# Second context pair's projections split around the first pair's masked products, and products ahead of transposes

## Chip, cores and metric

The kernel runs on one core of a Trainium2 chip. The metric is device time of one execution in microseconds (us), median of the runs shown. Engines are called PE (TensorE, matrix products), DVE (VectorE), ACT (ScalarE), POOL (GpSimd) and SP (SyncE, which issues loads).

## What is computed

A backbone of two layers over 512 latent tokens of width 1024 with a prefix of 256 context tokens. Layer 0 mixes with a bidirectional RWKV-7 recurrence over 16 heads of width 64, next to a gated short convolution; layer 1 is a convolution module. The change touches the recurrence over the context tokens, whose state at the end starts the recurrence over the latents:

```python
def wkv_scan(S0, r, decay, k, v, kk, a, reverse):
    def step(S, inp):
        r_t, w_t, k_t, v_t, kk_t, a_t = inp
        sa = jnp.einsum("bhvk,bhk->bhv", S, -kk_t)
        S = (S * w_t[:, :, None, :]
             + sa[..., None] * (kk_t * a_t)[:, :, None, :]
             + v_t[..., None] * k_t[:, :, None, :])
        return S, jnp.einsum("bhvk,bhk->bhv", S, r_t)
    ...
# k, v are projections of the normed tokens (h @ w_in), mixed with both neighbours:
    k = k + (centred_shift(k) - k) * mu_rkv[1]
    v = v + (centred_shift(v) - v) * mu_rkv[2]
```

Each scan runs forward and backward. Outside the recurrence, the conditioning needs `s @ mod_w[i] + mod_b[i]`.

## The kernel before

The scan is worked in chunks of 64 tokens. Two heads of 64 fill the 128 partitions, so 16 heads make 8 head pairs `p`. For the context (4 chunks), two head pairs are taken together: four states `sts[0]` to `sts[3]`, called context pairs here; context pair `b` holds head pairs `2b` and `2b+1`. The latents follow as eight more states. In names `c0` is context pair 0, `l0` latent pair 0, `z` (0, 1) the direction.

Steps of a context pair, by function:

- `prep_ctx`: key and value projections of both head pairs. `project` does the context tokens (PSUM tile `pc…`, 24 products of 256 columns) and then the latents with the same weights (`pl…`, 24 products of 512 columns; the result is stored in DRAM by POOL for later). Weights arrive as float32 and are split into a high and a low part (ACT cast `wh…`, DVE subtraction `wl…`), hence three products for each. `shifted` clears the PSUM tile: ACT L405, DVE L406 and L408. The tags `mm0` and `mm1` take turns, one bank each, so `pck3` takes the bank of `pck2`.
- `light`: decay, key normalisation and the operands `AR` and `BK` of both directions, on ACT and DVE.
- `heavy`: by letters. A, the masked products `pac…` of AR and BK (PE), cleared through the mask into E by DVE (L646); B, transposes `pbc…` of BK (PE), copied to BKt by ACT (L659); N, copies of parts of E to Nt (ACT, L665). A string in `HEAVY` gives their order: first entry for context pairs, second for latent pairs. `pv` turns the values (`pvc…`). A and B use the tag `at`, two banks in all.
- `solve`: an inverse by 31 rank-one steps on DVE (L697, L703, L705), then `merge`: DVE transposes `kdmc` and `amc`, and small products `uh<-amc` and `uh<-kdmc` on PE that complete E.
- `chain_ctx`: the recurrence over chunks (`zoc…`, `uh…`).

`rest()` is a side job in 17 steps, called between other steps: it loads pieces of `mod_w` (POOL) and multiplies them (`mpb…`, `uh<-mwr`); after the eighth and the last product `rested` copies, transposes (`mr…`, L948) and adds. `fills` writes projections that no pair needs yet (`plr…`, `pza…`); they stand between the pairs' steps.

The order on each engine is not the order of the code: a scheduler at build time takes instructions by priority, which follows the code, and by when it expects operands to be ready. Each engine then runs its list strictly in that order and waits where an operand or a buffer is missing. Buffers come from pools by tag; a tile waits for the last reader of the one whose place it takes.

In the code, the second context pair was prepared after the first one's merge:

## Time and profile before

| | |
|---|---|
| median of 3 runs | 1410.81 us (1405.18 to 1412.49) |
| profiled execution | 1408.22 us |
| its span | 1406.5 us |
| PE busy | 1344.4 us, 96% |
| DVE, ACT busy | 979.9 us (70%), 746.7 us (53%) |
| granted PE clock, mean | 0.986 of full |

The span is what the hardware profiler saw from the first to the last instruction; the time also holds start and end around it. The four context pairs fill the time from about 110 to 440 us, latent pairs follow to 940 us, then layer 1. A row of the timeline gives the start, the duration, engine, line, operation, output<-inputs, and in brackets the idle time before it and what ended that. PE rows overlap since products are pipelined: what a block takes is read from start to start.

### The profile page before, as it was taken

Reading aid. Unit: us, or ns where it says so; the run is one execution under the profiler, and the core shown is the slowest. Engines: PE = TensorE matmul, PEld = TensorE weight load, DVE = VectorE, ACT = ScalarE, POOL = GpSimd, SP = SyncE. Lnnn points to the kernel's source line nnn. Section 1 sums busy time; section 2 is a strip of 40 time slices with the busy share of each in tenths; the row PEclk is TensorE's granted clock in tenths of the full one; section 3 lists DMA queues with packets and bytes.
Section 4 is the critical chain, followed back from the end, with each engine's and each line's share of the span. In section 5 each row is a group of like instructions: output and inputs, shape, how many; then the busy total and the mean of one; then the engine's idle time right before and its main releaser. Section 6 shows DMA issues by size and latency. Waiting matters only on the chain. (4 is left out here: it accounts for less than half of the span.)

```text
span 1406.5 us, 29747 instructions
## 1 busy us (share of the span) xinstructions
PE 1344.4 (96%) x11921; PEld 1001.9 (71%) x11921; DVE 979.9 (70%) x2290; ACT 746.7 (53%) x1516; POOL 127.5 (9%) x263
## 2 busy tenths in 40 slices
PE   5898999999999998999999999999999999999998
PEld 1665767777767766666666666678777787788886
DVE  2775687877899789999999988556754644534333
ACT  4746355645757464665757656446752432453322
POOL 4022210001011001101011000010000000000000
PEclk9998899999999999999999999999999999999999
DMA  9864441223233222222222222459712312133222
GB/s 335 233 201 150 149 129 58 68 91 89 76 110 97 83 62 84 78 71 84 63 87 75 64 59 86 160 184 326 253 32 89 120 45 75 61 105 101 94 93 88
DMA packets 137707, 158.55 MB, mean 113 GB/s; under 512 B 15503, under 2 KB 104223, under 8 KB 137449
## 3 DMA queue, kind: packets, MB, share of 16 engines
q1 hardware_dynamic: 121104, 106.47, 24.2%
q0 software_dynamic: 15856, 49.12, 10.8%
q8 instruction: 94, 1.54, 0.4%
q10 hardware_dynamic: 608, 1.06, 0.2%
q14 instruction: 45, 0.37, 0.1%
HBM read 138.33 MB, written 18.28 MB: 111 GB/s over the span
## 5 line engine op out<-in xcount | busy, mean ns | idle before, releaser
L57 PE MATMUL o<-wh,y 128*128 128x512 f32 x248 | 79.6, 397 | 0.0
L703 DVE TENSOR_TENSOR xtmpl<-Xl,Yl 128x126 f32<-128x126 f32 (+22 forms) x248 | 62.1, 250 | 3.0
L705 DVE TENSOR_TENSOR Yl<-Yl,xtmpl 128x126 f32<-128x126 f32 (+22 forms) x248 | 62.0, 250 | 2.9
L1212 ACT CAST ah<-a 64x512 fp32r<-64x512 f32 x32 | 19.8, 618 | 74.1 <-DVE a L1207 73.8
L57 PE MATMUL zol<-UV,E 64*64 64x64 f32 (+1 forms) x1024 | 54.0, 221 | 0.0
L57 PE MATMUL pal<-ARl,BKl 64*128 64x128 f32 x512 | 46.7, 304 | 7.3 <-DVE E L646 6.1
L57 PEld LDWEIGHTS o<-wh,y 128*128 128x128 f32 x248 | 45.9, 188 | 9.5
L57 PE MATMUL zol<-Hl,ARl 64*64 64x64 f32 x896 | 50.2, 230 | 1.2 <-DVE Hl L818 0.9
L811 ACT COPY UV<-uh 64x128 f32<-64x128 f32 x128 | 33.2, 260 | 33.0 <-PE uh L57 26.7
L57 PEld LDWEIGHTS zol<-Hl,ARl 64*64 64x64 f32 x896 | 35.0, 133 | 21.4 <-issue 17.4
L57 PE MATMUL o<-wl,y 128*128 128x512 f32 x124 | 49.3, 397 | 1.0 <-DVE wl L130 1.0
L57 PEld LDWEIGHTS pal<-ARl,BKl 64*128 64x128 f32 x512 | 36.8, 197 | 18.0 <-issue 6.6
L130 DVE TENSOR_TENSOR wl<-wr,wh 128x1024 fp32r<-128x1024 f32 x28 | 34.2, 1222 | 20.8 <-ACT wh L129 20.7
L57 PEld LDWEIGHTS uh<-UV,BKt 128*64 128x64 f32 x704 | 26.3, 137 | 30.8 <-ACT UV L811 24.9
L1207 DVE TENSOR_TENSOR a<-pu,a 128x512 f32<-128x512 f32 x16 | 11.0, 690 | 49.2 <-PE pu L57 46.9
L646 DVE TENSOR_TENSOR E<-pal,maskE 128x512 f32<-128x512 f32 x64 | 43.1, 684 | 2.3 <-PE pal L57 2.0
L57 PEld LDWEIGHTS zol<-UV,E 64*64 64x64 f32 (+1 forms) x1024 | 42.4, 136 | 2.5 <-ACT UV L811 2.0
L1164 DVE SCALAR_TENSOR_TENSOR pr<-px,dbe,What 119x512 f32<-119x512 f32 x32 | 22.6, 746 | 26.6 <-PE px L57 26.6
L129 ACT CAST wh<-wr 128x1024 fp32r<-128x1024 f32 x28 | 29.6, 1057 | 19.4 <-DMA wr<-in_ev_w_out_dram 10.1
L57 PE MATMUL uh<-UV,BKt 128*64 128x64 f32 x704 | 36.3, 232 | 3.6 <-ACT UV L811 2.4
L818 DVE SCALAR_TENSOR_TENSOR Hl<-uh,PCl,HPl 128x64 f32<-128x64 f32 x112 | 26.4, 276 | 17.1 <-PE uh L57 7.2
L57 PEld LDWEIGHTS uh<-Ol,E 64*64 64x64 f32 x512 | 19.9, 133 | 25.3 <-ACT Ol L805 18.9
(980 smaller groups left out, 4206.2 us busy)
## 6 DMA issues: line engine op xcount, KB each, us to landing
wr<-in_ev_w_out_dram SPq DMA_DIRECT2D x28, 512.0 KB, 5.2
mwr<-in_mod_w_dram POOLq DMA_DIRECT2D x28, 256.0 KB, 4.0
ectx<-in_mod_w_dram SPq DMA_DIRECT2D x12, 512.0 KB, 7.2
wrv<-in_ev_w_in_dram SPq DMA_DIRECT2D x16, 256.0 KB, 3.0
ectx<-in_mod_w_dram POOLq DMA_DIRECT2D x16, 256.0 KB, 4.2
wrr<-in_ev_w_in_dram SPq DMA_DIRECT2D x16, 256.0 KB, 2.9
wrza<-in_ev_w_in_dram SPq DMA_DIRECT2D x16, 256.0 KB, 2.9
wrcg<-in_ev_w_in_dram SPq DMA_DIRECT2D x16, 256.0 KB, 2.8
```

The lines of the kernel that those rows point to most:

```text
L57: env["pe"] = T.matmul(o, lhsT, rhs, start=start, stop=stop)
L129: S.copy(hi, raw)
L130: env["lo"].tensor_tensor(out=lo, in0=raw, in1=hi, op=ALU.subtract)
L646: st["ev"].append(V.tensor_tensor(out=E[:, h, z * NLAT + c0 : z * NLAT + c0 + m, :], in0=pas[h], in1=maskE[:, z * (1 + h) : z * (1 + h) + ...
L703: V.tensor_tensor(out=tv, in0=X[:, :i, i : i + 1].to_broadcast([P, i, m]), in1=Y[:, i : i + 1, c0:].to_broadcast([P, i, m]), op=ALU.mult)
L705: V.tensor_tensor(out=Y[:, :i, c0:], in0=Y[:, :i, c0:], in1=tv, op=ALU.add)
L811: u_ = S.copy(UV[ZR[1 - h], i : 2 * nch - i : 2 * nch - 1 - 2 * i, ZR[h]], uh[ZR[1 - h], 0:2, :])
L818: h_ = V.scalar_tensor_tensor(out=Hn[:, z, :], in0=uh[:, 2 + z, :], scalar=PC[z][:, i : i + 1], in1=HP[:, z, :], op0=ALU.mult, op1=ALU.add)
L1164: V.scalar_tensor_tensor(out=pr[s][:NPROD], in0=px[s][:NPROD], scalar=dbe[:, 0:1], in1=What[:, n * 512 : n * 512 + 512], op0=ALU.add, op1= ...
L1207: V.tensor_tensor(out=a, in0=pp[1], in1=a, op=ALU.mult)
L1212: S.copy(ahl[s][hr], a[hr])
```

## The change

The call that prepares the second context pair is split in two: the keys (`kinds=(1,)`) are written ahead of the first pair's `heavy`, the values (`kinds=(2,)`) behind its `solve`. For every context pair, `heavy` writes A and N ahead of B.

```diff
-HEAVY = ("BAN", "ANBV")
+HEAVY = ("ANB", "ANBV")
...
     light(sts[0])
+    sts.append(prep_ctx(1, rest, kinds=(1,), inner=rest))
     heavy(sts[0])
     sts[0]["pv"]()
     solve(sts[0])
+    prep_ctx(1, rest, st=sts[1], kinds=(2,), inner=rest)
     merge(sts[0])
-    sts.append(prep_ctx(1, rest, inner=rest))
     rest()
```

What this makes of the engines' lists is shown at three places. Rows that repeat are left out.

First, PE where the first pair's `heavy` stands; `plk2` is the last key projection of head pair 2 over the latents, `pck3` that of head pair 3 over the context, `pbc00…` and `pbc01…` the transposes of directions 0 and 1, `pac00…` and `pac01…` the products. Before:

```order
L57 MATMUL plk2_1335<-hlh_117,wlk21_1284 128x512
L57 MATMUL mpb_1365<-ectx_121,s2_71 2x512 x4
L621 MATMUL pbc001_1027<-ident_60,BKc00_988 128x64
...
L621 MATMUL pbc011_1047<-ident_60,BKc01_1018 128x64
...
L57 MATMUL pck3_1387<-hctx_120,whk30_1376 128x256 x2
L57 MATMUL pck3_1387<-hctx_120,wlk30_1377 128x256
L57 MATMUL pac0001_1067<-ARc00_987,BKc00_988 128x64
...
L57 MATMUL pac0101_1087<-ARc01_1017,BKc01_1018 128x64
...
L57 MATMUL pvc0_1110<-ctr_106,vc0_635 64x64 x16
L948 MATMUL mr0_1321<-ident_60,mrow0_1320 128x128 x2
```

And now:

```order
L948 MATMUL mr0_1069<-ident_60,mrow0_1068 128x128 x2
L57 MATMUL plk2_1083<-hlh_117,whk21_1031 128x512
...
L57 MATMUL mpb_1113<-ectx_121,s2_71 2x512 x4
L57 MATMUL pac0001_1213<-ARc00_987,BKc00_988 128x64
...
L57 MATMUL pck3_1135<-hctx_120,whk30_1124 128x256 x2
...
L57 MATMUL plk3_1171<-hlh_117,whk30_1124 128x512
...
L57 MATMUL pac0101_1233<-ARc01_1017,BKc01_1018 128x64
...
L57 MATMUL pcv2_1397<-hctx_120,whv20_1386 128x256 x2
...
L621 MATMUL pbc001_1257<-ident_60,BKc00_988 128x64
...
L621 MATMUL pbc011_1277<-ident_60,BKc01_1018 128x64
...
L57 MATMUL pvc0_1296<-ctr_106,vc0_635 64x64 x16
```

The products of direction 0 now come first, the whole of `pck3` and `plk3` stands between them and those of direction 1, and the transposes stand within the value projection `pcv2`; the `mr` transposes stand within `plk2`.

The same place on DVE, from the first direction's BK on. Before:

```order
L596 TENSOR_TENSOR BKc_988<-kdc_982,iPc_977 128x8x64
L561 SCALAR_TENSOR_TENSOR Pc_1005<-scm,sg 128x528
L130 TENSOR_TENSOR wlv_1464<-wrv_1462,whv_1463 128x512
L588 SCALAR_TENSOR_TENSOR ARc_1017<-kkc_960,Pc_1005 128x8x64
...
L595 SCALAR_TENSOR_TENSOR BKc_1018<-ac_1002,iPc_1007 128x8x64
L406 SCALAR_TENSOR_TENSOR kc_1275<-pck_1288,hmu,kc_1275 128x255
...
L408 SCALAR_TENSOR_TENSOR kc_1275<-pck_1288,hmu,kc_1275 128x255
L408 SCALAR_TENSOR_TENSOR lk_1360<-plk_1335,hmu,lk_1360 128x511
L646 TENSOR_TENSOR ectx<-pac_1067,maskE 128x512
...
L646 TENSOR_TENSOR ectx<-pac_1087,maskE 128x512
...
L697 STREAM_TRANSPOSE Xc_1131<-Nt 128x32x32
```

And now:

```order
L561 SCALAR_TENSOR_TENSOR Pc_1005<-scm,sg 128x528
L952 TENSOR_TENSOR gate_74<-mr_1069,cols_68 128x8
...
L955 MEMSET uh_123 128x512
L130 TENSOR_TENSOR wlv_1387<-wrv_1385,whv_1386 128x512
...
L588 SCALAR_TENSOR_TENSOR ARc_1017<-kkc_960,Pc_1005 128x8x64
...
L408 SCALAR_TENSOR_TENSOR kc_1023<-pck_1036,hmu,kc_1023 128x255
...
L646 TENSOR_TENSOR ectx<-pac_1212,maskE 128x512
...
L408 SCALAR_TENSOR_TENSOR kc_1023<-pck_1135,hmu,kc_1023 128x255
...
L408 SCALAR_TENSOR_TENSOR lk_1196<-plk_1171,hmu,lk_1196 128x511
L646 TENSOR_TENSOR ectx<-pac_1233,maskE 128x512
...
L697 STREAM_TRANSPOSE Xc_1317<-Nt 128x32x32
```

The second direction's operands (L588 to L595) still stand ahead of L406 and L408; the clearing of `pck3` and `plk3` now comes ahead of the inverse (L697) and not within it, as do the sums on `mr` (L952).

Second, PE at the first pair's merge. Before:

```order
L57 MATMUL plv3_1596<-hlh_117,wlv31_1556 128x512
L57 MATMUL mpb_1365<-ectx_121,s2_71 2x512 x4
L57 MATMUL uh1_124<-amc0_1199,ectx_121 32x32 x32
L57 MATMUL mpb_1365<-mwr3_500,s2_71 2x512
...
L57 MATMUL plr0_1857<-hlh_117,whr00_1846 128x512
...
L57 MATMUL uh1_124<-kdmc0_1198,Pmc0_1200 32x32 x32
```

And now:

```order
L57 MATMUL plv3_1519<-hlh_117,wlv31_1479 128x512
L57 MATMUL mpb_1113<-ectx_121,s2_71 2x512 x4
L57 MATMUL plr0_1857<-hlh_117,whr00_1846 128x512
...
L57 MATMUL uh1_124<-amc0_1554,ectx_121 32x32 x32
L57 MATMUL plr0_1857<-hlh_117,whr01_1852 128x512
...
L57 MATMUL pza0_1899<-hlh_117,whza00_1888 128x512
...
L57 MATMUL uh1_124<-kdmc0_1553,Pmc0_1555 32x32 x32
L57 MATMUL mpb_1113<-mwr3_500,s2_71 2x512
```

Of the fill `plr0`, 21 of 24 products now stand ahead of the merge's first small products.

Third, PE at the first latent chain, where the masked products of latent pair 1 stand as blocks of 16 (`pal11…`, `pal10…`). Before:

```order
L57 MATMUL pal1101_4906<-ARl11_4738,BKl11_4739 128x128
...
L57 MATMUL pal1111_4918<-ARl11_4738,BKl11_4739 128x128
...
L57 MATMUL plr7_5144<-hlh_117,whr70_5133 128x512
...
L57 MATMUL pal1001_4930<-ARl10_4708,BKl10_4709 128x128
```

And now:

```order
L57 MATMUL pal1101_4906<-ARl11_4738,BKl11_4739 128x128
...
L57 MATMUL plr7_5144<-hlh_117,whr70_5133 128x512
...
L57 MATMUL pal1111_4918<-ARl11_4738,BKl11_4739 128x128
...
L57 MATMUL plr7_5144<-hlh_117,wlr70_5134 128x512
...
L57 MATMUL pal1001_4930<-ARl10_4708,BKl10_4709 128x128
```

Eight of the `plr7` products moved from behind the second block to ahead of it. Shortly behind this place, in the middle of conv_branch(0), the lists of before and now become the same on all engines and stay so to the end.

## The prediction, made before the changed kernel ran

> **What bounds the kernel now.** I read the page first, for the busy shares and the clock row.

> ```profile
> span 1406.5 us, 29747 instructions
> PE 1344.4 (96%) x11921; PEld 1001.9 (71%) x11921; DVE 979.9 (70%) x2290; ACT 746.7 (53%) x1516; POOL 127.5 (9%) x263
> PEclk9998899999999999999999999999999999999999
> ```

> TensorE (PE) works 96% of the span, so moved work pays in two ways only: less PE idle time, or less work done while PE's clock is low. Slices 4 and 5 (from 105 to 176 us) show such a clock. The chain of waits begins at 913 us and says nothing of the stage that the change touches. So I asked for PE's busy time in stretches. The columns are the stretch, its length, PE's busy time and instruction count, the granted clock, and the DMA share and rate.

> ```profile
> 126.30:134.10 7.80, 3.13 (x42) 0.89 0.69 213
> 134.10:152.90 18.80, 18.73 (x130) 0.50 0.04 15
> 181.60:219.34 37.74, 36.92 (x395) 1.00 0.30 89
> 246.16:400.00 153.84, 149.34 (x1551) 1.00 0.29 88
> 400.00:500.00 100.00, 92.44 (x1001) 0.97 0.30 88
> ```

> PE idles for 4.67 us between 126.3 and 134.1, and then works for 18.7 us at half clock. Elsewhere up to 400 us its idle time is small. Half-microsecond stretches show the clock falling at 132.43 and returning at 152.92, 20.49 us later. Two later falls, at 456.66 and 535.16, lie whole multiples (95 and 118) of 3.413 us from the first. Cutting the trace into slices of that length, on that grid, gives:

> ```profile
> 129.02:132.43 3.41, 0.00 (x0) 1.00 0.96 303
> 132.43:135.85 3.42, 2.80 (x22) 0.50 0.18 71
> 135.85:139.26 3.41, 3.41 (x30) 0.50 0.22 82
> 149.50:152.92 3.42, 3.42 (x38) 0.50 0.01 2
> 152.92:156.33 3.41, 3.41 (x18) 1.00 0.38 119
> 453.25:456.66 3.41, 1.59 (x32) 1.00 0.47 138
> 456.66:460.07 3.41, 2.06 (x17) 0.50 0.27 77
> 460.07:463.49 3.42, 3.42 (x10) 0.50 0.20 77
> 463.49:466.90 3.41, 3.41 (x34) 1.00 0.20 77
> 531.75:535.16 3.41, 1.78 (x24) 1.00 0.19 38
> 412.48:415.90 3.42, 2.52 (x92) 1.00 0.23 49
> ```

> In these rows the clock halves after a slice in which PE was busy for at most 1.78 us, and not after one with 2.52. A slice full of 512-column projection products (460.07) brings it back. The slices after 132.43 were full too, but of 64-column products mixed with projections, and it took six of them. The rows behind the idle piece:

> ```profile
> 126.30 1.04 PE L57 MATMUL mpb<-ectx,s 128*2 128x512 f32 x8
> 132.75 1.11 PE L621 MATMUL pbc<-ident,BKc 64*128 64x64 f32 x16 [4.05 <-ACT BKc L597]
> 134.10 0.79 PE L57 MATMUL pck<-hctx,whk 128*128 128x256 f32 x2 [0.24 <-DVE kc L408]
> 143.46 3.67 PE L57 MATMUL pac<-ARc,BKc 64*128 64x64 f32 x30
> 129.50 0.69 DVE L588 SCALAR_TENSOR_TENSOR ARc<-kkc,Pc 128x512 f32<-128x512 f32 x1 [1.49 <-ACT Pc L564]
> 133.57 0.47 DVE L408 SCALAR_TENSOR_TENSOR kc<-pck,hmu,kc 128x255 f32<-128x255 f32 x1
> ```

> The first pair's second transposes wait 4.05 us for the second direction's BK, which VectorE (DVE) and ScalarE (ACT) are still making. Behind them the next key projection waits for DVE's L408 at 134.04, since it takes the PSUM bank that L408 reads.

> **The change, part by part.** No instruction is added or removed; all is order.

> *The idle piece moves and hardly shrinks.* PE now has four `mr` transposes and the first masked products ahead of the wait. Rows that price the moved blocks, all at full clock:

> ```profile
> 160.21 0.51 PE L57 MATMUL pcv<-hctx,whv 128*128 128x256 f32 x2
> 163.25 1.04 PE L57 MATMUL mpb<-mwr,s 128*2 128x512 f32 x8
> 164.22 0.50 PE L57 MATMUL plv<-hlh,whv 128*128 128x512 f32 x1
> 169.91 1.04 PE L57 MATMUL mpb<-ectx,s 128*2 128x512 f32 x8
> 181.60 1.20 PE L57 MATMUL uh<-amc,ectx 32*32 32x32 f32 x64
> 186.87 0.44 PE L948 MATMUL mr<-ident,mrow 128*128 128x128 f32 x2
> 207.27 2.00 PE L57 MATMUL pac<-ARc,BKc 64*128 64x64 f32 x30
> 204.94 0.71 PE L621 MATMUL pbc<-ident,BKc 64*128 64x64 f32 x16
> 214.39 1.15 PE L57 MATMUL pvc<-ctr,vc 64*64 64x64 f32 x32
> ```

> From starts to starts a context projection takes 3.04 us, the `mpb` block 0.97, a latent projection 5.69. From 126.3: `mr` 0.9, `mpb` 1.0, 32 masked products 2.1 (30 take 2.00), so PE runs dry at 130.3. The next key projection still needs L408 at 134.04, and DVE's order still has the second direction's five operations ahead of it (they start at 129.50, held by ACT). The `mr` sums, the memset and one weight split now precede them, in DVE's 1.49 us wait; were that cover too short, L408 would slip by what sticks out. So PE idles 3.7 us: **-1.0** (between -4.7, if the wait went, and 0).

> *The slow stretch shortens.* Slice 129.02 to 132.43 then holds 1.3 us of PE work, under 1.78, so the clock still falls at 132.43. But what follows at 134.1 is undiluted projection: slice 135.85 to 139.26 is full of `pck`, and I expect full clock from 139.26, as after 460.07. Before, the slow slices held 2.80 + 3.41 + 3.41 + 3.42 + 3.41 + 3.42 = 19.87 us of work, 9.9 lost. Now 5.2 us of work, 2.6 lost: **-7.3** (-9.9 if the clock holds, 0 if six slices stay).

> [...]

> *The first inverse starts no earlier.* Its rows on DVE, and three groups of DVE's work between 149.9 and 182.5 us that stands between the inverse's steps (the last columns are busy time, mean, idle time before and its releaser):

> ```profile
> 150.01 1.97 DVE L697 STREAM_TRANSPOSE Xc<-Nt 128x1024 f32<-128x1024 f32 x1 [1.97 <-ACT Nt L665]
> 180.83 0.71 DVE L712 STREAM_TRANSPOSE amc<-kdmc 128x512 f32<-128x512 f32 x1
> L130 DVE TENSOR_TENSOR wlv<-wrv,whv 128x512 fp32r<-128x512 f32 x3 | 2.1, 692 | 0.7 <-ACT whv L129 0.7
> L952 DVE TENSOR_TENSOR gate<-mr,cols 128x8 f32<-128x8 f32 x1 | 0.2, 165 | 1.2 <-PE mr L948 1.2
> L955 DVE MEMSET uh<- 128x512 f32 x1 | 0.5, 485 | 0.6 <-ACT mrow L946 0.6
> ```

> Before, the second masked products ended at 147.1, the inverse began 2.9 us later, and `amc` was ready at 181.54, 31.5 after that. Now those products come behind the whole of pair 3's key: 134.1 + 3.04 + 0.97 + 5.69 + 0.97 + 2.1 + 2.6 (slow) = 149.4; inverse at 152.3. DVE no longer does the key's evacuations, the `mr` work with its waits (1.8 us) and two of three weight splits between the inverse's steps, but one more value evacuation and one more split; I take 4.5 us off the 31.5 (between 2 and 6): `amc` at 179.3. PE arrives after 149.4 + 2 x (3.04 + 5.69) + 4 x 0.97 + 1.42 (`pbc`) + 1.15 (`pvc`) + 21 of 24 `plr` products, 4.98 = 178.3. **+1.0** of new wait (0 to 3). What waits behind it on PE is the rest of fill 0, then the merge; `mpb` behind those.

> *All four context pairs: products before transposes.* Pair 1: PE idled 0.8 us in 181.6 to 219.3, among transposes waiting for BK. Those go, but its second transposes now wait for BKt copies that stand behind ACT's Nt copies: 0 (-0.8 to +0.8). In pairs 2 and 3 the inverse starts earlier; PE idled only 4.5 us in the 154 us from 246 on, so I take 0 (-2 to +2).

> *The burst of latent masked products.*

> ```profile
> 458.01 2.08 PE L57 MATMUL pal<-ARl,BKl 64*128 64x128 f32 x16 [2.01 <-DVE E L646]
> ```

> Before, this block followed one of its kind directly. Eight `plr` products (1.9 us) now stand between the two and would fill the 2.01. The idle time may turn up ahead of the next block, as DVE must clear the banks anyway; the slow slices (5.48 us of work, 2.7 lost) are the rest. I take half of the slow loss: **-1.4** (-4.7 to +2).

> *Queues.* On SP the last `wrr` and two `wrk` loads pass the eight small `lwc2` loads, which pair 2 needs only near 247 us; on POOL the second `Yc` load passes behind one `lv` store and is needed some 25 us later. Both at nothing; without that cover each costs one DMA, 2 to 4 us.

> **Sum:** -1.0 - 7.3 + 1.0 - 1.4 = -8.7 us. The profiled execution took 1408.22 us, 1.7 beyond its span; it becomes 1399.5. The median of the runs, 1410.81, stands 2.6 above the profiled one, so I forecast 1402.1.

> **The rivals.**

> [...]

> *The clock comes back as late as before*, because projection at half clock with `mpb` between doesn't count as busy. For it: slice 135.85 was full and did not help. Against it: 460.07 did. The -7.3 goes: 1409.4, no change that shows. Here the change doesn't do what it could.

> *The wait for `amc` lowers the clock again.* It decides from 1.6 us of waiting inside one slice (3.41 - 1.78); my 1.0 is near. The merge's 32-column products are then what follows. Two slow slices, as at 456.66, give back 3.4: 1405.5. Six, as at 132.43, cost 10.2: 1412.3, slower than before. It needs more than five to be slower.

> **How the numbers follow.** Forecast 0.40, clock never falls 0.15, late return 0.20, `amc` with two slow slices 0.15, with six or a worse wait 0.10. Low end: -8.7, the 2.6, 3.3 more from the burst, 1.0 without the wait for `amc` and 0.8 from pair 1, in all -16.4: 1394. The high end is the last case, 1412. About 0.5%, 7 us, is what a measurement can tell; the border is at 1403.8. The forecast, with some 3 us of its own spread, passes it in 0.7 of its cases: faster 0.28 + 0.15 = 0.43; of the last case 0.04 reaches beyond +7, and 0.05 goes to waits that I have not seen: 0.09. What is left, 0.48, is no change.

> **What would show it.** Right: PE idle of 3 to 4 us ends in `pck` <- DVE `kc` L408 near 134; half clock for two slices, not six; inverse starts near 152; `uh` <- `amc` waits about 1 us near 179; the same places lie 7 us earlier from 220 on. Wrong: half clock past 143, a wait over 2 us at `amc`, or PE idle beyond 12 us between 246 and 500.

## The result: 0.7% faster, some two thirds of it clock

| | before | changed |
|---|---|---|
| median | 1411.65 us (8 runs, 1405.18 to 1420.59) | 1400.88 us (8 runs, 1399.12 to 1403.82) |
| profiled execution's span | 1406.5 us | 1397.5 us |
| PE idle, 100 to 1000 us | 36.0 us | 32.4 us |
| lost to the low clock, 100 to 1000 us | 15.2 us | 8.7 us |

The ratio is 0.9932 (95% interval 0.9903 to 0.9961). The last two rows are summed over half-microsecond stretches: what PE does not work of each, and its work times what is missing of the full clock. Between these two executions 3.6 us of idle time went and 6.5 us of loss at the low clock; the span fell by 9.0 us. The page of the changed kernel:

```profile
span 1397.5 us, 29749 instructions
PE 1340.0 (96%) x11921; PEld 997.8 (71%) x11921; DVE 981.6 (70%) x2290; ACT 747.6 (53%) x1516; POOL 127.0 (9%) x263
PEclk9999999998999999999999999999999999999999
```

The low digits of slices 4 and 5 in the clock row are gone; a new one stands in slice 10 (from 314 us). PE in slices of the clock's grid, in the changed kernel:

```profile
128.07:131.48 3.41, 2.05 (x36) 1.00 0.71 203
131.48:134.89 3.41, 0.48 (x2) 0.50 0.69 257
134.89:138.31 3.42, 3.42 (x18) 0.50 0.22 81
138.31:141.72 3.41, 3.41 (x23) 1.00 0.00 1
336.26:339.67 3.41, 2.93 (x89) 1.00 0.49 150
339.67:343.09 3.42, 3.42 (x60) 0.50 0.02 5
346.50:349.91 3.41, 3.41 (x12) 0.50 0.02 5
446.00:464.00 18.00, 15.96 (x149) 1.00 0.32 103
```

Two slow slices follow the gap, not six. Three new ones (339.67 to 349.91) follow a slice in which PE worked for 2.93 of 3.41 us. The stretch from 446 to 464 holds the burst of latent masked products; its clock stays full. The rows of the timeline that the prediction named:

```profile
134.41 0.76 PE L57 MATMUL pck<-hctx,whk 128*128 128x256 f32 x2 [4.29 <-DVE kc L408]
179.76 1.20 PE L57 MATMUL uh<-amc,ectx 32*32 32x32 f32 x64 [1.13 <-DVE amc L712]
130.33 0.69 DVE L571 TENSOR_TENSOR kdc<-kdc,kc 128x512 f32<-128x512 f32 x1
133.79 0.47 DVE L408 SCALAR_TENSOR_TENSOR kc<-pck,hmu,kc 128x255 f32<-128x255 f32 x1
152.08 2.03 DVE L697 STREAM_TRANSPOSE Xc<-Nt 128x1024 f32<-128x1024 f32 x1 [1.97 <-ACT Nt L665]
131.05 0.47 ACT L405 ACTIVATE kc<-pck,omu 128x256 f32<-128x256 f32 x1 [0.19 <-DVE kdc L571]
450.82 1.16 PE L57 MATMUL pal<-ARl,BKl 64*128 64x128 f32 x16 [0.68 <-DVE E L646]
453.00 0.50 PE L57 MATMUL plr<-hlh,whr 128*128 128x512 f32 x1 [0.52 <-DVE lr L408]
```

The row before the last two holds something that the prediction missed. ACT's clearing of `pck2` (L405) waits for DVE's L571. The two share no PSUM bank: L571 is the last reader of `kc0`, the first pair's keys, and `kc1` takes its buffer. The last two rows are PE's waits at the burst of latent masked products; the 2.01 us between two blocks before are gone.

### The profile page after: what moved, and what is told of

The parts are those of the page before. It is cut to its first block, busy times and chain, and to the rows that moved or that the text cites. A ratio compares the mean times of both kernels' runs of the same rounds, so it can differ in the third digit from the quotient of the medians.

```text
span 1397.5 us, 29749 instructions
## 1 busy us (share of the span) xinstructions
PE 1340.0 (96%) x11921; PEld 997.8 (71%) x11921; DVE 981.6 (70%) x2290; ACT 747.6 (53%) x1516; POOL 127.0 (9%) x263
## 3 DMA queue, kind: packets, MB, share of 16 engines
q0 software_dynamic: 15856, 49.12, 10.6%
## 4 chain that ended last, share of the span: by engine, by line
PE 72%; DVE 14%; ACT 6%; issue 4%; DMA 4%; SPq 0%; POOL 0%; DVEq 0%; ACTq 0%; POOLq 0%
PE pu L57 13%; PE pz L57 6%; PE f L57 6%; PE uh L57 5%; PE zol L57 4%; PE pcg L57 4%; PE plk L57 3%; PE o L57 3%; PE pxb L57 3%; PE plv L57 2%; PE pza L57 2%; PE plr L57 2%; DVE E L646 2%; PE pck L57 2%; PE zoc L57 2%
## 5 line engine op out<-in xcount | busy, mean ns | idle before, releaser
L57 PE MATMUL o<-wh,y 128*128 128x512 f32 x248 | 79.7, 397 | 0.0
L57 PE MATMUL zol<-UV,E 64*64 64x64 f32 (+1 forms) x1024 | 54.1, 221 | 0.0
L57 PEld LDWEIGHTS o<-wh,y 128*128 128x128 f32 x248 | 45.9, 188 | 9.5
L57 PE MATMUL zol<-Hl,ARl 64*64 64x64 f32 x896 | 50.2, 230 | 1.0 <-DVE Hl L818 0.5
L57 PE MATMUL o<-wl,y 128*128 128x512 f32 x124 | 49.5, 399 | 0.9 <-DVE wl L130 0.9
L57 PEld LDWEIGHTS zol<-Hl,ARl 64*64 64x64 f32 x896 | 35.0, 133 | 21.2 <-issue 17.3
L57 PE MATMUL pal<-ARl,BKl 64*128 64x128 f32 x512 | 44.5, 292 | 5.2 <-DVE E L646 5.2
L57 PEld LDWEIGHTS uh<-UV,BKt 128*64 128x64 f32 x704 | 26.3, 137 | 30.0 <-ACT UV L811 23.7
L130 DVE TENSOR_TENSOR wl<-wr,wh 128x1024 fp32r<-128x1024 f32 x28 | 34.2, 1223 | 19.2 <-ACT wh L129 18.3
L57 PEld LDWEIGHTS pal<-ARl,BKl 64*128 64x128 f32 x512 | 34.8, 187 | 16.1 <-issue 5.9
L57 PEld LDWEIGHTS zol<-UV,E 64*64 64x64 f32 (+1 forms) x1024 | 42.4, 136 | 2.5 <-ACT UV L811 2.0
L646 DVE TENSOR_TENSOR E<-pal,maskE 128x512 f32<-128x512 f32 x64 | 43.1, 683 | 0.2
L129 ACT CAST wh<-wr 128x1024 fp32r<-128x1024 f32 x28 | 29.6, 1057 | 20.8 <-PE o L57 11.4
L57 PE MATMUL uh<-UV,BKt 128*64 128x64 f32 x704 | 36.3, 232 | 3.0 <-ACT UV L811 2.3
L57 PEld LDWEIGHTS uh<-Ol,E 64*64 64x64 f32 x512 | 19.9, 133 | 25.6 <-ACT Ol L805 18.8
```

The source lines that it names most:

```text
L57: env["pe"] = T.matmul(o, lhsT, rhs, start=start, stop=stop)
L129: S.copy(hi, raw)
L130: env["lo"].tensor_tensor(out=lo, in0=raw, in1=hi, op=ALU.subtract)
L646: st["ev"].append(V.tensor_tensor(out=E[:, h, z * NLAT + c0 : z * NLAT + c0 + m, :], in0=pas[h], in1=maskE[:, z * (1 + h) : z * (1 + h) + ...
```

## Experiments

Theory A came from the first two profiles. In a slice of 3.413 us I counted the columns that PE's products streamed, each product's columns times the share of the 128 rows that its operands fill (a 64-column product on 64 rows counts 32), spread from its start to the next start, or to its own end where that comes first; "weighted columns" below. Twelve more runs followed, two of them repeats.

### The changed kernel again

> The changed kernel once more, unaltered, for a second profile. Theory A (what PE streams decides the clock: in a slice of 3.413 us columns count, each by the share of the 128 rows that its operands fill; the clock falls below some 1,550 to 1,900 of them, and comes back above some 2,400 to 2,950): the fall behind the gap near 130 to 134 comes again and lasts two slices, since that gap is longer than a slice wherever the grid lies; the falls after slices that were partly busy (near 340 and 530) depend on where the grid lies and may be gone or moved. Ratio to before 0.990 to 0.996. Rival B (the slow stretches belong to fixed places of the program): all three come again, at 131, 340 and 531, with 2, 3 and 1 slices.

No edit. Ratio 0.9931 (0.9904 to 0.9958). Its profile, in slices:

```profile
129.29:132.70 3.41, 0.00 (x0) 1.00 0.83 302
132.70:136.12 3.42, 3.27 (x15) 0.51 0.22 81
255.57:258.98 3.41, 3.14 (x96) 1.00 0.34 88
258.98:262.40 3.42, 3.42 (x77) 0.51 0.20 77
```

The gap makes the clock fall again, here for one slice, since that one was full of `pck3`. The fall at 340 is gone, another at 259 has come (two slices), and others are at 460 and 525. So theory A's part on the grid holds, and B, with fixed places, does not. One execution's slow stretches elsewhere are no property of the order alone.

### Each part of the change alone

```diff
 # split_only: the changed kernel with
-HEAVY = ("ANB", "ANBV")
+HEAVY = ("BAN", "ANBV")
 # order_only: the kernel before with
-HEAVY = ("BAN", "ANBV")
+HEAVY = ("ANB", "ANBV")
```

> Only the split of the second pair's preparation; HEAVY as before (transposes first). PE then waits in the first pair's second transposes and again for L408, but pck3 and plk3 follow undiluted, as in the changed kernel. Theory A: the wait near 129 to 134 stays at 4 to 5 us, half clock for two or three slices (6.8 to 10.2 us) instead of six, 4 to 7 us gained; no slow stretch near 340, since pairs 1 to 3 have the old order. Ratio 0.993 to 0.997. Rival B (the gain comes from products ahead of transposes, for all four pairs): ratio 0.998 to 1.002, and five or six slow slices stay.

> Only HEAVY ANB for the four context pairs; the second pair's keys stay behind the first merge in the code. On PE pac of both directions then come ahead of pck3, and the pbc transposes stand among the products of pck3. Theory A: a gap of 2.5 to 4.5 us near 130 to 134; behind it pck3 (24 x 256 columns) and 32 transposes (64 columns on 64 rows) give 7,200 weighted columns in some 7.5 us at half clock, 3,200 a slice, just above what brings the clock back: two to four slow slices, 2 to 6 us gained, ratio 0.995 to 0.999, and perhaps the slow stretch near 340 as in the changed kernel. Rival B (only the split with its undiluted projection brings the clock back): six slow slices, ratio 0.999 to 1.003.

Split only: 0.9981 (0.9962 to 1.0000). Order only: 0.9961 (0.9938 to 0.9984). Slices of the split alone:

```profile
130.78:134.20 3.42, 0.58 (x13) 1.00 0.95 338
134.20:137.61 3.41, 2.68 (x14) 0.50 0.16 62
137.61:141.02 3.41, 3.41 (x18) 0.50 0.10 35
141.02:144.44 3.42, 3.42 (x20) 0.99 0.32 91
```

Its timeline, at the gap and at the first merge:

```profile
133.62 0.62 PE L621 MATMUL pbc<-ident,BKc 64*128 64x64 f32 x13 [4.16 <-ACT BKc L597]
189.20 1.20 PE L57 MATMUL uh<-amc,ectx 32*32 32x32 f32 x64 [1.26 <-DVE amc L712]
```

Slices of the order alone:

```profile
133.20:136.61 3.41, 3.21 (x28) 0.50 0.03 10
136.61:140.02 3.41, 3.41 (x19) 0.50 0.20 77
140.02:143.44 3.42, 3.42 (x35) 1.00 0.00 0
```

Its gap in the timeline; the second masked products wait for DVE to clear the banks of the first:

```profile
133.40 4.18 PE L57 MATMUL pac<-ARc,BKc 64*128 64x64 f32 x32 [3.37 <-DVE ectx L646]
```

Each part alone brings two slow slices instead of six, as theory A had it; B, in either form, had five or six. The split's ratio falls short of its forecast and lies in B's range, though the trace has A's two slices. With transposes first, the masked products come last (from 149.5 us), the inverse starts later (at 159.44, where the kernel before has 150.01 and the order alone 140.88), and PE idles 8.6 us between 100 and 240 where the kernel before idles 6.1. So the split gains at the clock and gives part of it back in waits; the products ahead of the transposes keep the inverse early.

### Products first for the first pair alone

```diff
-        for x in HEAVY[lat]:
+        for x in (HEAVY[lat] if lat or not st["p"] else "BAN"):
```

> The changed kernel with products ahead of transposes for the first context pair alone; pairs 1 to 3 have transposes first again. Theory A: the place near 130 as in the changed kernel (gap 4.3, two slow slices). The slow stretch near 340 (three slices, 5 us lost), whose slice ahead held only products of 64 columns on 64 rows and of 32 columns, goes, because a plv block or transposes stand there as before; the burst near 450 may be slow again (2.7 lost). Ratio 0.989 to 0.994. Rival B (the new order gains in pairs 1 to 3 by less waiting): 2 to 5 us slower than the changed kernel, ratio 0.995 to 0.998.

0.9959 (0.9938 to 0.9980). There is no slow stretch near 340, but there are single slow slices at 409 and 453. PE idles 37.0 us between 100 and 1000, against 32.4 and 31.8 in the two profiles of the changed kernel; 3.0 of it lies at the burst near 450 (0.98 and 2.02), where the changed kernel has 1.2. Rival B is nearer: in pairs 1 to 3 the new order saves waiting that this kernel pays again. The intervals of the two ratios overlap, so that the difference itself, 0.3%, is not settled.

### The buffer of the second pair's keys

```diff
-            st["rkv"[which]] = t = w("rkv"[which] + "_", "rkv"[which] + st["nm"])
+            st["rkv"[which]] = t = w("r_" if which == 1 and b == 1 else "rkv"[which] + "_", "rkv"[which] + st["nm"])
```

Of all pairs, only the latent ones use the buffer of tag `r_`. The edit was made to the changed kernel (own_k) and to the kernel before (before_own_k).

> The changed kernel, with the second context pair's keys (kc1) in a buffer of their own instead of the first pair's, so that ACT and DVE may clear pck2 before the first pair's second direction has read kc0. On PE pck3 then stands ahead of the first masked products. Theory C (the gap near 130 to 134 is the wait for that one buffer: kc1 may not be written before L571 has read kc0, so L408, and with it pck3's bank, comes at 134): the gap of 4.3 us shrinks to under 1.3 us, with no fall of the clock there (2 us lost in the changed kernel): 4 to 6 us less than the changed kernel, ratio to before 0.987 to 0.992, if the wait for amc stays near 1 us. Rival D (the second direction's operands on DVE are the limit whatever the buffer): the gap stays at 3 to 4 us ahead of plk3 or of the second masked products, the clock falls, ratio 0.991 to 0.995.

> The kernel before, with only that buffer of its own for the second pair's keys. pck3 then stands among the first transposes on PE, and the first masked products among those of plk3. Theory C: the wait of 4 to 5 us near 129 to 134 goes to under 1.5, the clock doesn't fall there, and the six slow slices (9.9 us) go: 8 to 13 us less than before, ratio 0.990 to 0.995, as much as the changed kernel gained without any of its changes. Rival D: the wait stays near 4 us and the clock falls; with projection mixed in, two to four slow slices, ratio 0.994 to 0.999.

On the changed kernel 0.9887 (0.9852 to 0.9922), median 1393.08 against 1409.68 us; on the kernel before 0.9926 (0.9898 to 0.9954), 1396.99 us. Rows of own_k:

```profile
114.91 0.46 ACT L405 ACTIVATE kc<-pck,omu 128x256 f32<-128x256 f32 x1
127.02 0.50 PE L57 MATMUL pck<-hctx,whk 128*128 128x256 f32 x2
133.80 0.47 PE L57 MATMUL plk<-hlh,whk 128*128 128x512 f32 x1 [0.77 <-DVE lk L408]
```

And the slice in which the gap was:

```profile
132.34:135.76 3.42, 2.65 (x23) 1.00 0.88 262
```

Theory C holds in both. `pck2` is cleared at 115 instead of 131, `pck3` starts at 127.02 without a wait, 0.77 us of idle time is left, and the clock stays full. On the kernel before, this one line brings as much as the whole change, which is about what was lost around the gap there. Its profiled execution was the slowest of its twelve (1411.12 us), which shows the other side of the clock:

```profile
132.52:135.94 3.42, 3.42 (x29) 1.00 0.83 258
255.39:258.81 3.42, 2.58 (x79) 1.00 0.39 133
258.81:262.22 3.41, 3.41 (x68) 0.51 0.07 25
275.87:279.28 3.41, 3.41 (x43) 0.99 0.01 3
```

The place of the gap is clean, but a slice of small products at 255 started five slow ones, and another such at 341 five more.

A second version on the changed kernel cleared `pck2` and `plk2` at high priority as well:

```diff
+            with tc.high_priority() if nm == "k2" else nullcontext():
-            shifted(pc, rc, p, which)
+                shifted(pc, rc, p, which)
...
+        with tc.high_priority() if nm == "k2" else nullcontext():
-        shifted(pl, rl, p, which)
+            shifted(pl, rl, p, which)
```

> As the changed kernel with the buffer of its own, and the clearing of pck2 and plk2 at high priority, so that L406 and L408 of lk2 stand ahead of the second direction's operands on DVE; on PE pck3 and plk3 then stand ahead of all masked products. Theory C: no gap ahead of plk3 (under 0.5 us); DVE's second direction 1.4 us later, which is hidden behind plk3; inverse and the wait for amc as in own_k or up to 3 us worse, since the masked products come later. Ratio 0.986 to 0.992. Rival: the wait for amc grows by what the gap lost, ratio 0.990 to 0.994.

0.9886 (0.9853 to 0.9919), 1393.94 us: not to be told from own_k. The remaining 0.77 us went (no PE wait over 0.2 us from 126 to 145), and the wait for `amc` is 0.77 us, so its rival falls; there was nothing more to win at this place. Either version beats the kernel before. Beside the changed kernel (0.9932 and 0.9931) the intervals still overlap, though own_k's executions took 1391.54 to 1397.48 us and those of the changed kernel, in its two runs, 1397.12 to 1403.82.

### PE kept streaming through the gap

```diff
                             go(pas[h][:, c, :], kb(BK, h, c0 + c), AR[ZR[h], c0 + c, 0:x])
+                    if nm == "c0" and z == 0:
+                        last = env["pe"]
+                        for i in range(17):
+                            e = mm(uhs[1][:, 0:512], hlat[0][:, i % 8, 0:P], hlat[0][:, i % 8, 0:512], True, True)
+                            tc.add_manual_dep(e.ins, last.ins.name, ...)  # behind the one before on PE
+                            last = e
```

> The changed kernel with 17 products of 512 columns on 128 rows (3.9 us), whose result nothing reads, behind the first masked products, so that PE streams columns through the gap from 130.1 to 134.4. Theory A (streamed columns set the clock): no slow slice near 131; the place where pck3 starts stays within 0.3 us of the changed kernel, and everything behind it is 1.6 to 2.2 us earlier; ratio to before 0.989 to 0.994. Rival B (the clock falls there because of something else, for example the load on DMA or on the other engines at this place): two slow slices stay, the products end past 134.4, and it is 0 to 4 us slower than the changed kernel.

0.9894 (0.9862 to 0.9926), 1394.53 us. With seventeen more products that nobody reads, the kernel is not slower than without them:

```profile
129.41 4.17 PE L57 MATMUL uh<-hlh 128*128 128x512 f32 x17
133.80 0.47 PE L57 MATMUL pck<-hctx,whk 128*128 128x256 f32 x2 [0.22 <-DVE kc L408]
```

The slice there:

```profile
130.90:134.32 3.42, 3.20 (x16) 1.00 0.67 247
```

DMA is as busy at this place as it was (shares 0.67 here, 0.69 there), and the clock stays full: so it is PE's own streaming that counts. Beside the changed kernel the ratio is some 0.4% lower, where 1.6 to 2.2 us were expected; the intervals overlap, so that the gain itself is not shown by the times. The merge gets `amc` at 177.44, against 179.76 and 177.91 in the two profiles of the changed kernel.

### What counts: busy time, columns or rows

Three kernels of the same kind, for their clock rows alone, one execution each. Wide: 44 such products. Rows: 44 with operands on 16 rows. Narrow: 190 of 8 columns.

```diff
 # tail_rows, in the place of fill_wide's product
+mm(uhs[1][:, 0:512], hlat[0][0:16, i % 8, 0:P], hlat[0][0:16, i % 8, 0:512], True, True)
 # tail_narrow
+mm(uhs[1][:, 0:8], hlat[0][:, i % 8, 0:P], hlat[0][:, i % 8, 0:8], True, True)
```

> The changed kernel with 44 products of 512 columns on 128 rows behind the first masked products, whose result nothing reads: 10.2 us at full clock, from 130 to 140, which covers the gap and 6 us more. Theory A (in a slice of 3.413 us columns count, each by the share of the 128 rows its operands fill; full clock stays above 2,630 of them and returns above 2,780): full clock throughout, no fall between 126 and 150; the block takes 10.2 us. Rival B (busy time decides): the same.

> The same 44 products of 512 columns, with operands on 16 of the 128 rows. PE is as busy and streams as many columns, but they count for an eighth: 940 a slice at full clock, 510 at half. Theory A: the clock falls after the first slice that is filled with them (between 133 and 137) and stays low until the block has ended and a slice of pck3 and plk3 has passed: the block takes 15 to 19 us instead of 10.2, three to six slow slices. Rival B (busy time, or columns without regard to rows): full clock, 10.2 us.

> The changed kernel with 190 products of 8 columns on 128 rows, of which the order puts 176 behind the first masked products and 14 behind plk3. PE is busy throughout: by the nearest rows (16 transposes in 0.71 us, 44 ns each; 64-column products 62 ns) 8 to 11 us at full clock. They count 8 columns each, 450 to 620 a slice. Theory A: the clock falls within the block (between 130 and 137) and stays low to its end and for the slice behind it, four to seven slow slices. Rival B (busy time): full clock throughout, as PE never stands still.

The scheduler put 20 of the 44 into the gap and 24 behind `plk3`. The blocks in the timeline, wide and then rows:

```profile
129.86 4.85 PE L57 MATMUL uh<-hlh 128*128 128x512 f32 x20
145.17 5.73 PE L57 MATMUL uh<-hlh 128*128 128x512 f32 x24
```

```profile
129.71 7.02 PE L57 MATMUL uh<-hlh 16*128 16x512 f32 x20
149.72 8.27 PE L57 MATMUL uh<-hlh 16*128 16x512 f32 x24
```

The first slow slice behind the first block, and the first at full clock again:

```profile
131.93:135.35 3.42, 3.42 (x10) 0.50 0.44 166
142.17:145.59 3.42, 3.42 (x19) 1.00 0.24 66
```

Narrow, the block in the timeline:

```profile
129.16 34.30 PE L57 MATMUL uh<-hlh 128*128 128x8 f32 x176
```

Its slices:

```profile
129.49:132.90 3.41, 3.41 (x33) 1.00 0.97 333
132.90:136.32 3.42, 3.42 (x18) 0.50 0.23 86
163.62:167.03 3.41, 3.41 (x17) 0.50 0.00 0
167.03:170.45 3.42, 3.42 (x23) 0.99 0.00 0
```

The wide block keeps full clock. The same number of columns on 16 rows lets it fall, with PE busy in every slice: 7.02 + 8.27 = 15.3 us for the two blocks, against 10.6, and eight slow slices in two groups, more than the three to six expected, since the block was split. The narrow block stayed at half clock for ten slices of full busy time. Its length was misjudged: 34.3 us for 176 products, where 8 to 11 us at full clock was expected. From start to start they took 112 ns in the first slice, at full clock, and 213 ns at half.

Over all fourteen profiles, the two from which the weights were taken among them, 100 to 610 us, by weighted columns. The edges are read off these same slices:

| slice at full clock, weighted columns | clock fell behind it | stayed |
|---|---|---|
| below 1,500 | 30 | 0 |
| 1,500 to 2,600 | 17 | 71 |
| above 2,600 | 1 | 1,846 |

| slice at half clock | stayed low | came back |
|---|---|---|
| below 2,600 | 59 | 0 |
| 2,600 to 3,020 | 5 | 9 |
| above 3,020 | 0 | 39 |

How the columns of a product at a slice's border are shared out moves single slices by some per cent, a few across the edges. The one fall above 2,600 (2,954, in the kernel with 16 rows, a slice with the `mpb` block of 2 stationary columns) I can't explain.

### The kernel before, again

> The kernel before once more, for a second profile. Theory A: the gap near 129 to 133 makes the clock fall wherever the grid lies, and the mixture behind it (pck3 thinned with transposes and masked products; 1,020 to 2,400 weighted columns a slice at half clock) keeps it low for four to seven slices, until past the value products near 149. Other falls may lie elsewhere than at 456 and 535. Rival (six slices were an accident of that execution's grid): two or three slices.

```profile
129.77:133.19 3.42, 0.00 (x0) 1.00 0.97 328
133.19:136.60 3.41, 3.09 (x22) 0.50 0.08 31
150.25:153.67 3.42, 3.42 (x32) 0.50 0.01 2
153.67:157.08 3.41, 3.41 (x19) 1.00 0.42 135
```

Six slow slices again, on another grid, so the rival falls. In the first profile of before the six slices count 1,370, 1,112, 2,177, 1,581, 2,319 and 5,222: five below what brings the clock back, one above. The second profile has a fall that the first lacks, four slices from 208. The six were no accident of the grid but the mixture behind the gap.

## Why the prediction held, and where it did not

The forecast was 1402.1 us and the measured median 1400.88. By its terms, on the profiled execution:

- **The idle piece: -1.0 forecast, -0.4 measured.** PE ran dry at 130.12 (forecast 130.3) and went on at 134.41 (134.1). It ends in `pck3` behind L408, as said. The reason given, that DVE's order has the second direction's operands ahead of L408, was incomplete: `kc1` must wait for L571 in any order, and with a buffer of its own (own_k) L405 and L408 come ahead of these operands. The bound "-4.7, if the wait went" was right about what lay there, and own_k collected most of it.
- **The slow stretch: -7.3 forecast, -8.0 measured** (9.9 us lost before, 1.9 now; 1.6 in the second profile). Two slices, as said. The mechanism was named rightly: a slice of undiluted projection (134.89 to 138.31, 3.42 us of `pck3`) brought the clock back, and "late return" did not come.
- **The clock never falls:** it fell in both profiles of the changed kernel, behind slices with 2.05 and 0.00 us of work. No run shows the 2.6 us that the range counts for this: in the profiles of both kernels, of split_only and of order_only the clock fell at the gap, and in own_k and fill_wide, where it stayed full, no such gap was left (2.65 and 3.20 us of work in the slice). Nor is a full slice enough: in tail_rows and tail_narrow the clock fell behind slices in which PE was busy for all 3.41 us (128.52 to 131.93, 129.49 to 132.90), with products on few rows or of few columns, and in tail_narrow it stayed at half clock behind nine such slices in a row, from 132.90 to 163.62. The prediction was right that it falls, but its border of 1.78 us of busy time failed: the clock fell behind 2.05 and 2.93 us in the changed kernel and stayed behind 2.65 in own_k. Columns, not busy time, were the measure.
- **The inverse and the wait for `amc`: +1.0 forecast, 1.13 measured.** The inverse started at 152.08 (forecast 152.3), PE came to the wait at 178.6 (178.3) and got `amc` for 179.76 (179.3). That wait did not lower the clock in either profile; the rival that it would stays possible, since in fill_wide the same wait, of 1.15 us, was followed by a slow slice (178.7 to 182.1).
- **Pair 1: 0 forecast, about -1 measured.** PE's waits before, of 0.31 and 0.51 us in this pair and 0.51 at 221.58, have no counterpart over 0.15 us.
- **The burst at 453: -1.4 forecast, about -3.9 measured.** PE idled 3.17 of the 18 us from 450 to 468 before and 2.04 of those from 446 to 464 now, and the 2.7 us of slow clock went. The 2.01 us ahead of the second block went, as `plr` fills them, and only 0.52 turned up elsewhere, ahead of `plr`; the prediction had counted none of this gain. Over 440 to 500 us the gain is 5.4 us, 2.7 of it idle time; the second profile had one slow slice there (460 to 464), so it isn't settled either.
- **Pairs 2 and 3: 0 forecast.** This step failed. Idle time from 240 to 440 fell by 0.9 us (2.3 in the second profile), but slow slices cost 5.1 us (3.4), where before had none: the slice of 336.26 with small masked products and the 32-column merge counts 1,836. That the new order makes such falls likelier is not shown: before_own_k, with the old order, fell at 259 and 344, and the changed kernel's second profile has none at 340.

So the total came out by luck in part: the 4.2 us lost from 240 to 440, which the prediction had put at nothing, and 4.0 us more than forecast gained from 440 to 500 nearly cancel. The slow stretch, its largest term, was right by itself.

The time then follows, to within 4 us, from two numbers. The span less PE's idle time and less the low clock's loss, both from 100 to 1000 us, lies between 1354.1 and 1357.9 us in all kernels without added products (one execution each):

| kernel | span | idle | low clock | rest |
|---|---|---|---|---|
| before | 1406.5 | 36.0 | 15.2 | 1355.3 |
| before, again | 1411.5 | 36.2 | 21.2 | 1354.1 |
| changed | 1397.5 | 32.4 | 8.7 | 1356.4 |
| changed, again | 1395.9 | 31.8 | 9.3 | 1354.8 |
| split_only | 1406.0 | 40.1 | 9.4 | 1356.5 |
| order_only | 1399.9 | 32.4 | 10.9 | 1356.6 |
| first_only | 1400.0 | 37.0 | 7.5 | 1355.5 |
| own_k | 1390.4 | 27.1 | 8.5 | 1354.8 |
| own_k_early2 | 1389.4 | 29.8 | 1.7 | 1357.9 |
| before_own_k | 1409.3 | 32.4 | 22.1 | 1354.8 |

## What to carry to other kernels

When an engine waits, follow the releaser one step further than the instruction it names: here PE's wait for L408 was in truth one buffer with a single copy, and one line that gave it another was worth as much as the reordering (0.9926 beside 0.9932). Where PE is as busy as here (96% of the span), add up idle time and low clock apart. Here a wait cost its own length and then what the clock lost until a slice was full of wide products: 9.9 us over six slices in the kernel before, with 64-column products among the projections, and 1.9 over two in the changed kernel, with projections alone. So put projections of many columns, not small products, behind a wait that can't be avoided. And an execution's slow stretches are not those of the next: the changed kernel's clock fell at 339.67 in one profile and at 258.98 in the other, whose slices' borders lie 1.22 us later. Take a second profile before explaining one.
